# Fixed places of a state-space layer's side work in a dense matmul stream: some groups' state products and turned outputs stand one to three triples later

## The chip, the cores and the metric

One core of a Trainium2 chip runs the whole program. The metric is the device time of one execution in microseconds, as the median of several runs. One execution before was also taken by the hardware profiler; all rows shown here come from that one. Names of engines in the rows: PE is TensorE, PEld its weight loads, DVE is VectorE, ACT is ScalarE, POOL is GpSimd, SP is SyncE, which issues DMAs.

## The reference, cut to what matters

A token sequence of 512 x 1024 goes through one Mamba-2 layer, then one differential-attention layer, all in float32. The change lies in the Mamba-2 layer, which has 8 groups of 4 heads, 64 wide, with a state of 128:

```python
zxbcdt = rms_norm(x, norm_g) @ w_in            # z, x/B/C of 8 groups, dt
xbc = silu(causal_depthwise_conv(xbc, conv_w, conv_b))
# per chunk of the scan, per group g:
cb = einsum("blgn,bsgn->blsg", c_c, b_c)
y_diag = einsum("blsgr,bsgrp->blgrp", cb[..., None] * decay, x_c)
y_off = einsum("blgn,bgrpn->blgrp", c_c, state) * exp(acs)[..., None]
new_state = state * exp(acs[:, -1]) + einsum("blgn,blgrp->bgrpn", b_c, x_c * to_end)
...
y = y + d_skip * xs
y = gated_group_rms_norm(y, z, gate_norm_g)    # per group: y * silu(z), normed
return x + y @ w_out
```

## The kernel before

Float32 products are made as three matmuls of split operands (a high and a low part, `hi` and `lo`): `mm3`, line 259, called a **triple** here. The layer's projections are one dense stream of triples with a right side of 512 columns. `first_layer` (line 579) walks it by `order_a`: "z0 g0 g1 z1 g2 g3 z2 g4 o0 g5 z3 g6 g7 o1 o2 o3". A `z` item projects gate columns for two groups (into `pz`, then ScalarE's `zs`), a `g` item projects and convolves the x, B and C of one group (`pg`, then a scaling and three steps on VectorE into `xc`, with ScalarE around them), an `o` item is part of the output projection. Most items are 64 triples in two segments of weights. The weights come by SP's queue into `raw` (line 194), ScalarE makes `whi` and VectorE `wlo` of them, four instructions each for a segment, into three buffers in turn.

The work of the scan for group g is the generator `ssd` (line 618). It stops at each `yield` and is resumed at a fixed place: a number of triples, counted from the end of the group's own `g` item, out of the table `PLACES` (line 40). The columns of that table are groups 0 to 7. Its steps on TensorE are:

- `cb`: four products `pcb`.
- `bt`: three transposes `pbt`, which ScalarE copies into `bt`.
- `xt`: four transposes into `pxt_0` and four into `pxt_1`, which VectorE multiplies into `xdt` and `dx`; GpSimd makes `xe` of `xdt` (line 651).
- `st`: the state products `psA` and `psB` with `xe`, then `pyd`. The states `hst` go from ScalarE's copy of `psA` over GpSimd (line 662), VectorE, GpSimd (line 666) to VectorE.
- `o1`, `o2`: the products of states, `po`. Behind them `dx` is added up (GpSimd, line 701), gated, squared on ScalarE, and scaled by ScalarE into `tmp`.
- `y0`: the **turned outputs**: four transposes into `pyt_0`, four into `pyt_1`; ScalarE makes `yh` of each, VectorE `yl`.

The small PSUM tiles `pbt`, `pxt`, `psA`, `psB`, `pyd`, `po` and `pyt` share three banks in turn (`ss_bank`, line 96), so each of them waits until its bank's last tile has been read.

The decay tables `dec` have two buffers. `decays` (line 599) loads one by SP (line 606), GpSimd copies a piece (line 608), subtracts (line 610) and masks (line 611) it, four instructions each, and ScalarE takes the exponential of the whole table. The next load into a buffer waits until its last reader, among them line 666, is done.

TensorE's instructions run in the order in which they were recorded (`Ordered`, line 55; for all of them the profile shows line 70). The order on VectorE, ScalarE, GpSimd and SP is chosen by a scheduler when the program is built, and is then as fixed.

Of the kernel before, what the change touches and what calls it, by code (L numbers as in the profile page):

```python
# [38 lines left out]

PLACES = {  # L40
# [7 lines left out]
    "y2": (None,) * 7 + (72,),  # L48
}

# [1170 lines left out]
```

## Time and profile before

| what | value |
| --- | --- |
| median of 3 runs | 705.75 us (705.56 to 706.2) |
| profiled execution | 707.18 us, its span 705.4 us |
| TensorE busy | 696.1 us, 99% of the span |
| VectorE busy | 524.2 us, 74% |
| ScalarE busy | 426.3 us, 60% |
| GpSimd busy | 116.1 us, 16% |
| mean granted clock of TensorE | 0.998 |

The profile's times count from the start of the span. [...] Ends of matmuls are modelled, so a matmul's row of 0.39 us overlaps the next one, which starts 0.23 us after it.

### The profile page before, as it was taken

The page shows a single profiled execution, that of the slowest core. Times are in us where ns is not written, and L with a number is a line of the kernel's source. Part 1 is how long each engine was busy: PE and PEld are TensorE (multiplying, and loading weights), DVE is VectorE, ACT ScalarE, POOL GpSimd, SP SyncE. Part 2 cuts the span into 40 slices and gives each one's busy share as a digit, 9 for nine tenths or more (in the row PEclk, how much of TensorE's full clock was granted, in tenths as well). Part 3 has the DMA queues.
Part 4 walks back from the last instruction along what each step waited for, and adds up shares of the span by engine and source line. Part 5 has one row for each costly group of instructions (what it writes and reads, how often), then busy time and mean ns, then how long its engine had stood idle before and what let it go on. Part 6 is the DMA issues. An engine that isn't in the chain of part 4 may idle for free.

```text
span 705.4 us, 10468 instructions
## 1 busy us (share of the span) xinstructions
PE 696.1 (99%) x3838; PEld 580.7 (82%) x3838; DVE 524.2 (74%) x1181; ACT 426.3 (60%) x931; POOL 116.1 (16%) x158
## 2 busy tenths in 40 slices
PE   8999999999999999999999999999999999999996
PEld 7888788888878888888888888888888888888884
DVE  5499967799489679569995757557778757787776
ACT  6859663573654547536635258567777667665546
POOL 0008242502406025042110101000000000000002
PEclk9999999999999999999999999999999999999999
DMA  8654314214125323313222111513112221130103
GB/s 293 257 193 170 120 60 135 105 61 179 42 79 180 105 76 120 110 70 120 64 84 94 60 60 53 194 60 113 67 60 77 80 83 61 60 106 14 31 1 119
DMA packets 13491, 70.85 MB, mean 100 GB/s; under 512 B 1792, under 2 KB 3328, under 8 KB 6016
## 3 DMA queue, kind: packets, MB, share of 16 engines
q1 hardware_dynamic: 13008, 69.90, 27.6%
q8 instruction: 30, 0.49, 0.3%
q10 hardware_dynamic: 432, 0.28, 0.1%
q14 instruction: 21, 0.17, 0.1%
HBM read 68.02 MB, written 2.16 MB: 99 GB/s over the span
## 4 chain that ended last, share of the span: by engine, by line
PE 78%; DVE 8%; ACT 5%; DMA 4%; issue 3%; POOL 2%; SPq 0%; ACTq 0%; POOLq 0%; DVEq 0%
PE po L70 16%; PE pg L70 14%; PE pt L70 8%; PE pq L70 6%; PE pk L70 6%; PE pv L70 6%; PE pz L70 6%; PE pb L70 3%; DMA raw<-in_w_in 3%; PE sc L70 3%; DVE wlo L70 2%; ACT whi L70 2%; PE pc L70 2%; PE pyd L70 2%; DVE xc L70 1%
## 5 line engine op out<-in xcount | busy, mean ns | idle before, releaser
L70 DVE SCALAR_TENSOR_TENSOR wlo<-raw,prm,whi 128x512 fp32r<-128x512 f32 (+1 forms) x240 | 149.3, 672 | 54.0 <-ACT whi L70 53.7
L70 ACT ACTIVATE whi<-raw,prm 128x512 fp32r<-128x512 f32 (+1 forms) x240 | 133.2, 629 | 46.7 <-PE pg L70 12.0
L70 PE MATMUL pg<-a_hi,whi 128*128 128x512 f32 x256 | 102.8, 402 | 0.0
L70 PE MATMUL pg<-a_hi,wlo 128*128 128x512 f32 x256 | 99.9, 390 | 0.0
L70 PE MATMUL pg<-a_lo,whi 128*128 128x512 f32 x256 | 99.7, 389 | 0.0
L70 DVE SCALAR_TENSOR_TENSOR xc<-pg,prc,xc 128x511 f32<-128x511 f32 (+2 forms) x96 | 70.9, 743 | 12.3 <-ACT xc L70 11.2
L70 PEld LDWEIGHTS pg<-a_hi,wlo 128*128 128x128 f32 x256 | 48.1, 188 | 10.3
L70 PEld LDWEIGHTS pg<-a_hi,whi 128*128 128x128 f32 x256 | 48.2, 188 | 9.6 <-ACT zs L70 0.2
L70 PEld LDWEIGHTS pg<-a_lo,whi 128*128 128x128 f32 x256 | 48.1, 188 | 9.4
L70 PE MATMUL po<-whi,yh 128*128 128x512 f32 x128 | 51.2, 400 | 0.0
L70 PE MATMUL pz<-whi,a_hi 128*128 128x512 f32 x128 | 49.7, 397 | 0.3 <-ACT a_hi L70 0.3
L70 PE MATMUL po<-whi,yl 128*128 128x512 f32 x128 | 49.9, 390 | 0.0
L70 PE MATMUL po<-wlo,yh 128*128 128x512 f32 x128 | 49.9, 390 | 0.0
L70 PE MATMUL pz<-whi,a_lo 128*128 128x512 f32 x128 | 48.9, 390 | 0.0
L70 PE MATMUL pz<-wlo,a_hi 128*128 128x512 f32 x128 | 48.9, 389 | 0.0
L1026 POOL TENSOR_TENSOR ot<-x_tok,fg 128x512 f32<-128x512 f32 x4 | 5.0, 1284 | 246.8 <-DVE x_tok L70 246.8
L70 ACT ACTIVATE xc<-xc 128x512 f32<-128x512 f32 x32 | 20.2, 630 | 40.5 <-DVE xc L70 36.7
L70 ACT ACTIVATE xc<-pg,prc 128x512 f32<-128x512 f32 x32 | 24.8, 774 | 28.3 <-DVE pg L70 27.9
L70 DVE CUSTOM_DVE_ANT_0 s<-sc,bias 128x128 f32<-128x128 f32 (+3 forms) x64 | 29.4, 488 | 16.0 <-PE sc L70 15.5
L70 ACT ACTIVATE s<-s,mx 128x128 f32<-128x128 f32 (+3 forms) x64 | 35.6, 557 | 9.1 <-DVE mx L70 8.9
L651 POOL TENSOR_TENSOR xe<-xdt,tok 128x256 f32<-128x256 f32 x24 | 14.0, 613 | 159.3 <-DVE xdt L70 159.3
L70 ACT ACTIVATE tmp<-dx 128x256 f32<-128x256 f32 x32 | 13.1, 410 | 36.8 <-DVE dx L70 36.8
(237 smaller groups left out, 1651.1 us busy)
## 6 DMA issues: line engine op xcount, KB each, us to landing
raw<-in_w_in SPq DMA_DIRECT2D x22, 1024.0 KB, 4.9
raw<-in_w_kvqg SPq DMA_DIRECT2D x16, 1024.0 KB, 4.8
dec<-acs_d SPq DMA_DIRECT2D x8, 1024.0 KB, 5.1
raw<-in_w_out SPq DMA_DIRECT2D x8, 1024.0 KB, 4.9
raw<-in_w_bo SPq DMA_DIRECT2D x4, 1024.0 KB, 4.8
x_tok<-in_x SPq DMA_DIRECT2D x4, 512.0 KB, 9.0
out<-ot SPq DMA_DIRECT2D x6, 256.0 KB, 2.1
raw<-in_w_in SPq DMA_DIRECT2D x4, 256.0 KB, 4.9
```

The source lines that it names most:

```text
L70: i = op(*args, **kw)
L651: GP.tensor_tensor(out=xe[:, c], in0=xdt[:, c], in1=toe_tok[:, c, hs].unsqueeze(2).to_broadcast([P, R, HD]), op=ALU.mult)
L1026: GP.tensor_tensor(out=o, in0=y, in1=f, op=ALU.mult)
```

## The change

Fourteen of the table's numbers change. `st` of groups 0, 2 and 6 stands one or two triples later, `o1` and `o2` of group 0 three, `bt` of groups 1, 2, 3 and 6 two or three, `y0` of groups 0, 1, 2, 5 and 7 one to three. `cb` and `xt` keep their places.

```diff
--- before.py
+++ after.py
@@ -39,12 +39,12 @@
 
 PLACES = {
     "cb": (10, 2, 14, 14, 5, 5, 14, 12),
-    "bt": (10, 29, 21, 44, 35, 25, 21, 37),
+    "bt": (10, 32, 23, 47, 35, 25, 23, 37),
     "xt": (18, 35, 31, 52, 43, 36, 31, 43),
-    "st": (27, 47, 37, 63, 53, 47, 38, 53),
-    "o1": (31, 47, 46, 63, 53, 47, 46, 53),
-    "o2": (31, 52, 46, 69, 60, 52, 46, 58),
-    "y0": (61, 85, 76, 99, 89, 85, 69, 69),
+    "st": (29, 47, 39, 63, 53, 47, 39, 53),
+    "o1": (34, 47, 46, 63, 53, 47, 46, 53),
+    "o2": (34, 52, 46, 69, 60, 52, 46, 58),
+    "y0": (64, 87, 79, 99, 89, 87, 69, 70),
     "y2": (None,) * 7 + (72,),
 }
```

TensorE executes the same instructions in another order. The scheduler gives the other engines other orders as well. In the following rows the numbers behind a tile's name are counters, and some shift with the change (`tmp_797` and `tmp_810` are the same tile of group 0); a minus stands ahead of a row of before, a plus ahead of a row of after.

VectorE, behind group 0's `st`. Here `hst` and `dx` belong to group 0's states, `pg_2` and `xc` to the convolution of group 1, `wlo` to a later segment's weights:

```order
 L70 SCALAR_TENSOR_TENSOR wlo_655<-raw_652,prm,whi_654 128x512 x4
+L70 TENSOR_TENSOR pg_2_728<-pg_2_728,ar_row 128x512
+L70 SCALAR_TENSOR_TENSOR xc_790<-pg_2_728,prc,xc_790 128x511
+L70 SCALAR_TENSOR_TENSOR xc_790<-pg_2_728,prc,xc_790 128x510
 L70 TENSOR_TENSOR hst_757<-psA_758,hst_757 128x256
-L70 TENSOR_TENSOR dx_702<-pyd_1_799,dx_702 128x512
-L70 TENSOR_TENSOR hst_757<-psB_792,hst_757 128x256
-L70 TENSOR_TENSOR dx_702<-pyd_0_798,dx_702 128x512
-L70 TENSOR_TENSOR pg_2_728<-pg_2_728,ar_row 128x512
+L70 TENSOR_TENSOR dx_702<-pyd_1_812,dx_702 128x512
+L70 SCALAR_TENSOR_TENSOR xc_790<-pg_2_728,prc,xc_790 128x509
+L70 TENSOR_TENSOR dx_702<-pyd_0_811,dx_702 128x512
```

The scaling of `pg_2` and two convolution steps now stand ahead of the first `hst` add, the third one behind `dx`.

GpSimd, over the making of the third decay table, `dec_1217`, and the adds of group 0's `dx`:

```order
-L701 TENSOR_TENSOR dx_702<-dx_702,tmp_797 128x256
 L608 COPY dec_1217<-dec_1217 128x8
-L610 TENSOR_TENSOR dec_1217<-dec_1217,tok 128x512 x2
-L701 TENSOR_TENSOR dx_702<-dx_702,tmp_797 128x256 x2
-L610 TENSOR_TENSOR dec_1217<-dec_1217,tok 128x512 x2
-L611 AFFINE_SELECT dec_1217<-dec_1217 128x512 x4
-L651 TENSOR_TENSOR xe_1104<-xdt_1053,tok 128x256 x3
+L701 TENSOR_TENSOR dx_702<-dx_702,tmp_810 128x256
+L610 TENSOR_TENSOR dec_1217<-dec_1217,tok 128x512 x4
+L611 AFFINE_SELECT dec_1217<-dec_1217 128x512 x3
+L701 TENSOR_TENSOR dx_702<-dx_702,tmp_810 128x256 x2
+L611 AFFINE_SELECT dec_1217<-dec_1217 128x512
```

The copy of the table stands ahead of the first add; the second and third add stand behind the four subtractions and three of the four masks, and not between the subtractions.

ScalarE, around group 0's turned outputs and group 1's `bt`; `zs` are gates, `whi_1070` four pieces of weights:

```order
 L70 ACTIVATE zs_2_0_1028<-pz_2_990,ar_col 128x256
 L70 ACTIVATE zs_2_1_1030<-pz_2_990,ar_col 128x256
-L70 CAST yh_889<-pyt_0_891 128x512
-L70 CAST yh_889<-pyt_1_892 128x512
-L70 COPY bt_1051<-pbt_1047 128x384
 L70 ACTIVATE whi_1070<-raw_1068,prm 128x512 x4
 L70 ACTIVATE zs_3_0_1064<-pz_3_1003,ar_col 128x256
 L70 ACTIVATE zs_3_1_1066<-pz_3_1003,ar_col 128x256
+L70 COPY bt_1048<-pbt_1044 128x384
+L70 CAST yh_923<-pyt_0_925 128x512
+L70 CAST yh_923<-pyt_1_926 128x512
```

The three drains, `yh` twice and `bt`, stand behind the four `whi` and two more `zs`, with `bt` first.

TensorE, around group 2's turned outputs (`pyt`) and group 3's `pbt`; the minus rows of the same three stand nine matmuls, three triples, ahead of this piece:

```order
 L70 MATMUL pg_1_1860<-a_lo,whi_1599 128x512
 L70 MATMUL pg_1_1860<-a_hi,wlo_1600 128x512
+L70 MATMUL pbt_1882<-ident,xc_1420 128x128 x3
+L70 MATMUL pyt_0_1734<-ident,tmp_1628 128x128 x4
+L70 MATMUL pyt_1_1735<-ident,tmp_1628 128x128 x4
 L70 MATMUL pg_1_1860<-a_hi,whi_1599 128x512
 L70 MATMUL pg_1_1860<-a_lo,whi_1599 128x512
```

The eleven transposes stand behind three further triples of `pg_1`, in the same order among themselves. Group 0's `pyt` and group 1's `pbt` move in the same way by three triples, to three triples ahead of group 1's `pxt`.

## Rows read from the trace of the kernel before

**Rows 1.** Table by windows, whole core: stretch, length, each engine's busy us (instructions), granted clock, DMA share.

```profile
6.30:702.50 696.20, 691.63 (x3821) 576.64 (x3819) 523.06 (x1179) 423.40 (x925) 115.29 (x151) 1.00 0.28 99
702.60:705.40 2.80, 0.00 (x0) 0.00 (x0) 0.00 (x0) 0.00 (x0) 0.00 (x0) 0.50 0.46 158
```

**Rows 2.** TensorE's waits: waiting, releaser; total us, times, longest us.

```profile
PE psA L70 <- POOL xe L651: 0.4, 1, 0.4
...
PE pyt L70 <- ACT tmp L70: 0.3, 1, 0.3
```

**Rows 3.** Timeline of TensorE, `st` of groups 0 and 2: start, us, instruction, count.

```profile
73.56 0.39 PE L70 MATMUL pg<-a_hi,wlo 128*128 128x512 f32 x1
...
78.18 0.50 PE L70 MATMUL pg<-a_hi,whi 128*128 128x512 f32 x1
...
162.47 0.39 PE L70 MATMUL pz<-whi,a_lo 128*128 128x512 f32 x1
...
166.10 0.50 PE L70 MATMUL pz<-whi,a_hi 128*128 128x512 f32 x1
```

**Rows 4.** Timeline of TensorE, turned outputs of groups 0 and 2.

```profile
103.68 1.03 PE L70 MATMUL pyt<-ident,tmp 128*128 128x128 f32 x8
...
104.80 0.48 PE L70 MATMUL pz<-whi,a_hi 128*128 128x512 f32 x1
...
194.97 0.49 PE L70 MATMUL pbt<-ident,xc 128*128 128x128 f32 x3
...
197.52 0.47 PE L70 MATMUL pg<-a_hi,whi 128*128 128x512 f32 x1
```

**Rows 5.** Timeline of ScalarE, scaling ahead of group 2's turned outputs.

```profile
195.24 1.71 ACT L70 ACTIVATE tmp<-dx,y_y 128x256 f32<-128x256 f32 x4
```

**Rows 6.** Chain of waits between 102 and 116 us: start, us, what.

```profile
107.12 2.04 PE pg L70 x9
109.16 0.87 PE pxt L70 x8
```

**Rows 7.** Timeline of GpSimd, 72 to 100 us.

```profile
73.72 1.76 POOL L651 TENSOR_TENSOR xe<-xdt,tok 128x256 f32<-128x256 f32 x3 [5.28 <-DVE xdt L70]
...
87.34 0.19 POOL L608 COPY dec<-dec 128x8 f32<-128x8 f32 x1 [3.22 <-DMA dec<-acs_d]
...
94.23 2.39 POOL L611 TENSOR_SCALAR_AFFINE_SELECT dec<-dec 128x512 f32<-128x512 f32 x4
```

**Rows 8.** Timeline of VectorE, the add of `hst` in group 0.

```profile
78.61 0.41 DVE L70 TENSOR_TENSOR hst<-psA,hst 128x256 f32<-128x256 f32 x1
```

**Rows 9.** Page, part 5, VectorE's convolution steps: count, busy, mean ns, idle before.

```profile
L70 DVE SCALAR_TENSOR_TENSOR xc<-pg,prc,xc 128x511 f32<-128x511 f32 (+2 forms) x96 | 70.9, 743 | 12.3 <-ACT xc L70 11.2
```

**Rows 10.** Timeline of SP's queue, load of a decay table.

```profile
79.74 0.33 SPq L606 DMA_DIRECT2D dec<-acs_d  x1
```

**Rows 11.** Instructions touching `acs_d`: its transfers, issue to landing.

```profile
DMA to landing us min/median/max: 1.4/4.8/7.5
```

**Rows 12.** Timeline of ScalarE, 93 to 110 us.

```profile
93.93 1.28 ACT L70 ACT_TABLE_LOAD   x1
96.65 1.93 ACT L70 ACTIVATE dec<-dec 128x2056 f32<-128x2056 f32 x1 [1.44 <-POOL dec L611]
...
101.12 1.70 ACT L70 ACTIVATE tmp<-dx,y_y 128x256 f32<-128x256 f32 x4
...
105.17 0.82 ACT L70 ACTIVATE zs<-pz,ar_col 128x256 f32<-128x256 f32 x2
105.89 1.06 ACT L70 CAST yh<-pyt 128x512 fp32r<-128x512 f32 x2
106.83 0.50 ACT L70 COPY bt<-pbt 128x384 f32<-128x384 f32 x1
107.20 2.58 ACT L70 ACTIVATE whi<-raw,prm 128x512 fp32r<-128x512 f32 x4
```

**Rows 13.** Timeline of VectorE, `yl` of group 0.

```profile
106.50 1.29 DVE L70 TENSOR_TENSOR yl<-pyt,yh 128x512 fp32r<-128x512 f32 x2 [0.29 <-ACT yh L70]
```

## The prediction

> **What bounds the kernel now.** I read the table by windows first. Over the 696 us between the first microseconds and the last matmul TensorE is busy 691.63 us, at a granted clock of 1.00 [rows 1]. So the kernel is a stream of matmuls, and only two things can change its time: TensorE work added or removed, or holes in that stream. The change adds and removes no TensorE instruction, so everything here is about holes. The list of waits comes next. Besides two at the program's very start it holds two, both in the first layer: the products of group 0's states wait 0.4 us for a GpSimd product, and the turned outputs of one group wait 0.3 us for ScalarE [rows 2]. These entries understate the holes, because a matmul's end is modelled late. I size a hole by comparing start to start against the same block elsewhere.
>
> For group 0's states, the last dense matmul starts at 73.56 and the next one behind the block at 78.18, which is 4.62 us apart. For group 2 the same block lies between starts at 162.47 and 166.10, 3.63 us apart [rows 3]. **Hole one is 0.99 us.** For the turned outputs, eight `pyt` and three `pbt` transposes with nothing late take from 103.68 to 104.80, 1.12 us. At group 2's outputs they take from 194.97 to 197.52, 2.55 us [rows 4]. **Hole two is 1.43 us.** There the transposes keep pace with four ScalarE copies that run from 195.24 to 196.95 [rows 5].
>
> The unit of a place is a dense triple, three matmuls. The chain shows 9 of them in 2.04 us [rows 6], so one triple is 0.68 us.
>
> **Group 0's `st`, two triples later: -1.0 us.** The block would start 1.36 us after 73.79 (73.56 plus 0.227 for one matmul), at 75.15. GpSimd makes the three `xe` pieces from 73.72 to 75.48 [rows 7], about 0.59 each, so the two that `psA` reads are there at 74.9 and the third just as `psB` begins. The hole goes whole. If GpSimd slipped by half a microsecond, 0.5 of it would stay.
>
> **What hangs on that block's new place.** VectorE's order changes behind it. Before, the add of `hst` stands right behind four `wlo` and runs at 78.61 [rows 8]. Now the scaling of `pg_2` and two steps of the convolution stand ahead of it (the order of VectorE shows this), each convolution step 743 ns [rows 9], with a ScalarE step between. Taking the four at some 0.6 to 0.75 us each makes the add about 2.6 us late. TensorE hardly feels it: the block with `o1`, group 1's `cb` and `o2` starts at 75.15 + 3.5 + 5 x 0.68 = 82.05, its last two products, which need the second `hst` add, come more than a microsecond into it, and that add ends near 83.7; between 0 and 0.5 us could be missing, and I take 0, since a hole there would only shorten the wait of the next part. But the second `hst` product on GpSimd frees the buffer into which the next decay table is loaded, so SP's issue of that load, at 79.74 before [rows 10], moves to about 82.3. How long it then takes is open: these loads take 1.4 to 7.5 us, 4.8 in the middle [rows 11]. Before, this one was the slow one (79.74 to GpSimd's copy at 87.34 [rows 7]), issued right behind a weight load on SP. Issued 2.6 us later it finds that load mostly through, so I take the middle: landed at 87.1, as before. The slow end, 89.8, is a rival below.
>
> **Group 0's `y0` and group 1's `bt`, three triples later, with `xt` not moved: +3.7 us.** This is the largest term, and it is a new wait. Before, six triples lie between `pbt` and `pxt`, which starts at 109.16 by the chain [rows 6]; now three, 2.04 us. `pxt_0` needs the bank that ScalarE's copy `bt` empties, and `pxt_1` the bank that VectorE's `yl` of `pyt_0` empties, which itself waits for ScalarE's `yh`. Before, ScalarE did `yh` at 105.89 and `bt` at 106.83, ahead of the four `whi` at 107.20 [rows 12]. In the new order `bt`, `yh`, `yh` stand behind those four `whi` (2.58) and the two `zs` behind them (0.72 to the next start).
>
> When does ScalarE get there? GpSimd's new order puts the adds of `dx` 2 and 3 behind the four subtractions and three of the four selects. Before, GpSimd was busy without a gap from 87.34 to 96.62 [rows 7], 9.3 us; one add of about 0.7 us that ran earlier comes in as well. From 87.1 this ends at 96.8 to 97.1, the last add one select (2.39 / 4 = 0.6) before that, at 96.2 to 96.5. Then come a VectorE product and a ScalarE square, some 1 us, and a table load (1.28), so the exponential starts at about 98.6 and not at 96.65 [rows 12]. From there the old row gives 4.47 us to the `tmp` copies (101.12). One 0.54 us step has moved ahead of it, so 3.93: `tmp` from 102.5 to 104.2. Now in steps: four `whi` 2.5 to 106.7, `zs` 0.7 to 107.4, four `whi` 2.5 to 109.9, `zs` 0.7 to 110.6, `bt` 0.45 to 111.1, the first `yh` 0.5 to 111.6, `yl` 0.65 (half of 1.29 [rows 13]) to 112.25, and the second four transposes 0.44 (half of 0.87 [rows 6]) to 112.7.
>
> Undisturbed, with hole one gone, `pxt` would end at 109.0: 109.16 less 0.99, plus 0.87 for eight transposes [rows 6]. The wait is 112.7 less 109.0, **3.7 us**. Its upper bound is 4.4, if GpSimd ends 0.3 later and the square stands 0.4 behind other work. Its lower bound: even without a backlog ScalarE can't start the second four `whi` before the z segment whose buffer they take has ended. That was at 107.12 [rows 6]; less hole one and the 1.2 us of transposes that now come behind it, 104.9. Then 2.5 + 0.7 + 0.45 + 0.5 + 0.65 + 0.44 lead to 110.1, a wait of 1.1. I take 3.7, since each step of the long chain has its own row.
>
> **Group 2's `y0` and group 3's `bt`, three triples later: -1.4 us.** `pbt` goes to 197.0 in the old frame, and the four copies end at 196.95 [rows 5]. Hole two goes whole; if ScalarE came 0.7 us later here, half of it would stay. `pxt` of group 3 then stands five triples behind, 3.4 us, at 201.6. `pyt` ends at 198.2; `bt`, `yh` and `yl` (0.45, 0.5, 0.65), with a convolution step of 0.75 ahead of them on either engine, free its bank by 200.6 to 201.3: no new wait, but little to spare.
>
> **The rest: 0.** Group 1's `y0` and group 2's `bt`, as groups 5 and 6, move together by two triples, `pxt` eight triples behind them instead of ten; the drains behind `pyt` and `pbt` need under 4 us of those 5.4. `st` of groups 2 and 6 moves away from its producers. Group 7's `y0` moves by one triple, and its second half still follows its own drains.
>
> **Sum.** -1.0 + 3.7 - 1.4 = +1.3 us. The profiled execution took 707.18 (span 705.4), 1.43 above the median of 705.75; there the sum gives 708.5, and against the median **707.0**. A measurement of this kernel tells about 0.2%, 1.4 us, from no change: 704.3 to 707.2 is the same.
>
> **Rivals.** *The forecast's own case*, a wait at group 1's `pxt` of 1.1 to 4.4 us: -1.3 to +2.0, so 704.4 to 707.8. Chance 0.68: 0.44 of it within 0.2%, 0.24 slower, since the sum lies close to that bound.
>
> *The two holes close and nothing opens.* It would need ScalarE to come to `bt` about as early as before in spite of its order. Against it stands the fixed order; for it, that before, ScalarE was through with `yh` and `bt` at 107.3 [rows 12], 1.8 us ahead of `pxt`. Price: -1.0 - 1.4 = -2.4, so 703.3. Chance 0.14.
>
> *The decay load takes its long time from its later issue.* It lands at 89.8, 2.6 us after what I took, and GpSimd, the exponential and the whole ScalarE chain go with it; it decides as soon as the landing passes 87.5. +1.3 + 2.6 = +3.9, so 709.6. For it: the 7.5 us that this very load took before. Chance 0.10.
>
> *The wait is long enough for TensorE's clock to fall.* [...] Chance 0.08. [...]
>
> **How the numbers follow.** Faster 0.14 (the second case), same 0.44, slower 0.42 (0.24 of the forecast's case, 0.10 and 0.08). The range takes the forecast's case and the second one, 0.82: from 703.2 to 708.2, the upper end with 0.4 for what may stay of hole two. It leaves out the two slower rivals.
>
> **What would show it.** In the list of waits of the changed kernel `psA` is gone, and `pxt` of group 1 stands there for ScalarE's `bt` and VectorE's `yl` with 3 to 4 us in sum. On ScalarE's timeline `bt` and `yh` stand behind the second four `whi`, at about 111. The exponential starts near 98.6. Start to start, group 2's outputs take 1.1 us and not 2.55. If no `pxt` wait is there, the second case is right and my reading of ScalarE's order fails. If GpSimd's copy of the decay table comes after 88, the load was late. If the granted clock dips behind the wait, the last rival holds.

## The result and the profile after

| | median, us | span of the profiled execution, us |
| --- | --- | --- |
| before | 705.88 (705.51 to 706.94, 6 runs) | 705.4 |
| after | 710.08 (708.06 to 711.25, 6 runs) | 706.3 |

The ratio after to before is 1.0053, with an interval of 1.0042 to 1.0065: slower by about 4 us, where the forecast was 1.3 us and its range ended at 708.2. The profiled execution of before, at 707.18 us, lies above all six of its runs. That of after (span 706.3) is the shortest of its six, at a mean clock of 0.998. The other five had spans of 707.7 to 709.5 at a mean clock of 0.995 or 0.996. So this first profile shows the change with the clock held; what the other five have beside it is told by e1 below.

TensorE's waits in the profiled execution of after (waiting, releaser, total us, times, longest us). Beside two at the program's start the list holds only these; the two of [rows 2] are gone:

```profile
PE pxt L70 <- ACT bt L70: 2.3, 1, 2.3
...
PE pxt L70 <- DVE yl L70: 0.6, 1, 0.6
```

TensorE's timeline of after, at the three places that answer to [rows 3] and [rows 4] (start, us, instruction, count):

```profile
74.94 0.39 PE L70 MATMUL pg<-a_hi,wlo 128*128 128x512 f32 x1
...
78.57 0.50 PE L70 MATMUL pg<-a_hi,whi 128*128 128x512 f32 x1
...
107.76 0.39 PE L70 MATMUL pg<-a_hi,wlo 128*128 128x512 f32 x1
110.45 0.66 PE L70 MATMUL pxt<-ident,xc 128*128 128x128 f32 x4 [2.30 <-ACT bt L70]
111.66 0.66 PE L70 MATMUL pxt<-ident,xc 128*128 128x128 f32 x4 [0.56 <-DVE yl L70]
112.07 0.47 PE L70 MATMUL pg<-a_hi,whi 128*128 128x512 f32 x1
...
112.84 0.40 PE L70 MATMUL pg<-a_hi,whi 128*128 128x512 f32 x1
...
199.30 0.49 PE L70 MATMUL pbt<-ident,xc 128*128 128x128 f32 x3
...
200.42 0.48 PE L70 MATMUL pg<-a_hi,whi 128*128 128x512 f32 x1
```

Group 0's `st`: from 74.94 to 78.57, 3.63 us, against 4.62 in [rows 3]. Hole one is gone. Group 1's `pxt`: from the last dense matmul at 107.76 to the next at 112.07, 4.31 us; undisturbed that stretch is 1.02 us (108.52 to 109.54 in e6, a later profile of before, whose rows stand there). So TensorE waits 3.29 us there, in two pieces, 2.30 and 0.56 by the rows' own count. Group 2's outputs: from 199.30 to 200.42, 1.12 us, against 2.55 in [rows 4].

GpSimd in after, the copy of the decay table and the last two adds of `dx`, against [rows 7]:

```profile
86.51 0.54 POOL L608 COPY dec<-dec 128x8 f32<-128x8 f32 x1 [4.91 <-DMA dec<-acs_d]
...
93.70 1.43 POOL L701 TENSOR_TENSOR dx<-dx,tmp 128x256 f32<-128x256 f32 x2
```

ScalarE in after, against [rows 12]:

```profile
98.04 1.92 ACT L70 ACTIVATE dec<-dec 128x2056 f32<-128x2056 f32 x1
...
101.99 1.70 ACT L70 ACTIVATE tmp<-dx,y_y 128x256 f32<-128x256 f32 x4
...
106.76 2.55 ACT L70 ACTIVATE whi<-raw,prm 128x512 fp32r<-128x512 f32 x4
...
109.92 0.47 ACT L70 COPY bt<-pbt 128x384 f32<-128x384 f32 x1
110.28 1.09 ACT L70 CAST yh<-pyt 128x512 fp32r<-128x512 f32 x2
```

The table lands no later than before (copy at 86.51, before 87.34), though its load was issued later. The last add ends at 95.13, behind the subtractions and three of the masks; the exponential starts at 98.04, `tmp` at 101.99, the second four `whi` at 106.76, and only then `bt` at 109.92 and `yh` at 110.28.

Windows of after across the wait (stretch, length, busy us of TensorE and its weight loads, VectorE, ScalarE, GpSimd, then the granted clock):

```profile
108.00:110.40 2.40, 0.15 (x1) 0.00 (x0) 2.25 (x4) 2.40 (x7) 0.00 (x0) 1.00 0.85 287
110.40:112.00 1.60, 0.99 (x7) 0.76 (x8) 1.08 (x2) 0.97 (x2) 0.00 (x0) 1.00 0.99 307
```

In this one execution the clock stays at 1.00 through the wait.

### The profile page after: what moved, and what is told of

Same layout as the page of the kernel before. It is cut to its first block, busy times and chain, and to the rows that moved or that the text cites. A ratio compares the mean times of both kernels' runs of the same rounds, so it can differ in the third digit from the quotient of the medians.

```text
span 706.3 us, 10474 instructions
## 1 busy us (share of the span) xinstructions
PE 695.3 (98%) x3838; PEld 581.3 (82%) x3838; DVE 524.0 (74%) x1181; ACT 426.9 (60%) x931; POOL 117.6 (17%) x158
## 4 chain that ended last, share of the span: by engine, by line
PE 82%; issue 6%; DMA 3%; ACT 3%; DVE 3%; POOL 2%; SPq 0%; ACTq 0%; POOLq 0%
PE pg L70 18%; PE po L70 16%; PE pt L70 8%; PE pq L70 6%; PE pk L70 6%; PE pv L70 6%; PE pz L70 6%; PE pb L70 3%; PE sc L70 3%; PE pc L70 2%; PE pyd L70 2%; DMA x_tok<-in_x 1%; POOL dec L611 1%; DMA xt<-in_x_t 1%; PE pyt L70 1%
```

## The experiments

Runs e1, e5 and e6 are a kernel unchanged; the others are edits of the table of places alone. Theory A: the long runs of after come from TensorE's clock, which falls in the wait at `pxt`. Theory B: they come from a late decay load. Theories C and D, from the fifth run on, are on the size of the gain. C: the profiled execution of before was a long one, and most executions of before lack one of its two holes. D: both holes are always there.

**e1, the changed kernel again**

> The changed kernel once more. In its profiled execution group 1's pxt waited 3.3 us in all (its block took 4.17 us, 0.88 undisturbed), the granted clock stayed at 1.00, and the span was only 0.9 us over that of before; the timed runs were longer, at a mean clock of 0.996 and not 0.998. Theory A (the clock falls in that wait): again a median near 710, runs above 709 with a mean clock of 0.995 or 0.996, and a profile of such a run shows a granted clock below 1.00 in the microseconds behind the wait. Theory B (the decay load lands late in most runs): the long runs keep the clock of 0.998, or the profile shows GpSimd's copy of the table behind 88 us and a longer wait at pxt.

Measured: median 710.0 (709.33 to 711.26, 6 runs), all at a mean clock of 0.994 to 0.996; ratio 1.006 (1.0039 to 1.0081). This time the profiled execution was one of these, with a span of 708.1. Its windows, same columns as above:

```profile
109.00:111.00 2.00, 0.00 (x0) 0.00 (x0) 2.00 (x4) 2.00 (x5) 0.00 (x0) 1.00 0.76 266
111.00:112.00 1.00, 0.78 (x4) 0.71 (x4) 0.34 (x2) 1.00 (x3) 0.00 (x0) 0.58 0.97 401
...
113.00:114.00 1.00, 1.00 (x5) 0.90 (x4) 1.00 (x3) 0.00 (x0) 0.00 (x0) 0.50 0.87 360
114.00:115.00 1.00, 1.00 (x4) 0.77 (x4) 1.00 (x3) 0.00 (x0) 0.06 (x1) 0.71 1.03 434
115.00:116.00 1.00, 1.00 (x7) 0.79 (x5) 0.46 (x1) 0.00 (x0) 1.00 (x2) 1.00 0.18 74
```

TensorE's timeline in it:

```profile
108.10 0.39 PE L70 MATMUL pg<-a_hi,wlo 128*128 128x512 f32 x1
111.22 2.32 PE L70 MATMUL pxt<-ident,xc 128*128 128x128 f32 x8 [2.73 <-ACT bt L70]
113.19 0.78 PE L70 MATMUL pg<-a_hi,whi 128*128 128x512 f32 x1
113.77 0.63 PE L70 MATMUL pg<-a_lo,whi 128*128 128x512 f32 x1
...
114.61 0.40 PE L70 MATMUL pg<-a_hi,whi 128*128 128x512 f32 x1
```

GpSimd's copy of the decay table, and ScalarE's `bt`:

```profile
87.06 0.75 POOL L608 COPY dec<-dec 128x8 f32<-128x8 f32 x1 [4.70 <-DMA dec<-acs_d]
...
110.69 0.48 ACT L70 COPY bt<-pbt 128x384 f32<-128x384 f32 x1
```

From 109 to 111 us TensorE does nothing. At about 111.2 the granted clock goes to 0.50; by 115 it is 1.00 again. The eight transposes and the matmuls behind them run in between: the first dense one is followed 0.58 us later by the second (113.19, 113.77), where it is 0.32 us in after's first profile and 0.23 from one dense matmul to the next. From the last dense matmul to the first transpose it takes 3.12 us (108.10 to 111.22), in after's first profile 2.69 (107.76 to 110.45): 0.43 us are a longer wait. From there to the second triple's start at 114.61 it takes 3.39 us, in the first profile 2.39 (110.45 to 112.84): 1.00 us is the clock's. A third difference lies ahead of the wait: the block of group 0's `o1`, group 1's `cb` and group 0's `o2` takes 2.30 us start to start here (82.11 to 84.41) and 2.00 there, 0.30 more. The three make 1.73 of the 1.8 us between the two spans. So Theory A is shown for this execution; the decay table was copied at 87.06, 0.55 us behind the time of after's first profile, which speaks against B. For the other long runs of after the mean clock says the same, but what makes some of them up to 1.4 us longer than this one is open. Of the 23 runs of before beside e1 one, of 709.27 us, has a mean clock of 0.995 too; where its clock fell no profile shows.

**e2, group 1's `xt` three triples later**

```diff
-    "xt": (18, 35, 31, 52, 43, 36, 31, 43),
+    "xt": (18, 38, 31, 52, 43, 36, 31, 43),
```

> The changed kernel with group 1's xt three triples later (38 for 35), so that pxt stands six triples behind pbt as it did before. ScalarE's order up to bt and yh is the same as in the changed kernel. pxt then waits for the same drains (bt at 110.4, yl at 111.6), but only 1.1 to 1.2 us. Theory A: such a wait leaves the clock alone, mean clock 0.998: before's median 705.9 - 2.4 + 1.2 = 704.7. Theory B: the late load adds its 3 us here as well: about 708.

Measured: 706.42 (705.89 to 707.01, 12 runs), mean clocks of 0.997 to 0.999; ratio 1.0008 (0.9997 to 1.0018). TensorE's timeline and the window across the wait:

```profile
110.95 0.66 PE L70 MATMUL pxt<-ident,xc 128*128 128x128 f32 x4 [0.69 <-ACT bt L70]
112.16 0.66 PE L70 MATMUL pxt<-ident,xc 128*128 128x128 f32 x4 [0.56 <-DVE yl L70]
```

```profile
111.00:112.50 1.50, 0.94 (x7) 0.71 (x8) 1.08 (x2) 0.87 (x2) 0.00 (x0) 1.00 1.09 284
```

The drains come between those of the two profiles of after (`bt` at 110.43), but dense work covers most of the time: two waits of 0.69 and 0.56 us remain, the clock stays at 1.00 and 3.6 us of the loss are gone. By its clock and its waits this is Theory A's case. The time alone does not decide it: it lies 1.7 us above A's 704.7 and 1.6 below B's 708. The miss of A's number is the first sign that something else in the sum was wrong.

**e3, group 1's `xt` two triples earlier**

```diff
-    "xt": (18, 35, 31, 52, 43, 36, 31, 43),
+    "xt": (18, 33, 31, 52, 43, 36, 31, 43),
```

> The changed kernel with group 1's xt two triples earlier (33): the drains come at the same time, so the wait grows by 1.36 us to some 4.7 us, and so does the whole. With a clock that holds: 705.9 + 0.9 + 1.4 = 708.2. Theory A: the clock falls in every run, 0.996 or less, 711 to 712. Theory B: 711.4 (after's 710.1 + 1.4) at a mean clock of 0.998.

Measured: 712.22 (711.01 to 712.73, 6 runs), mean clocks of 0.993 to 0.995; ratio 1.0086 (1.0068 to 1.0105). The wait and the windows in its profiled execution:

```profile
111.42 2.32 PE L70 MATMUL pxt<-ident,xc 128*128 128x128 f32 x8 [4.95 <-ACT bt L70]
```

```profile
110.00:111.00 1.00, 0.00 (x0) 0.00 (x0) 1.00 (x2) 1.00 (x4) 0.00 (x0) 0.96 0.93 393
111.00:112.00 1.00, 0.58 (x3) 0.58 (x4) 0.34 (x2) 1.00 (x4) 0.00 (x0) 0.50 1.06 451
...
117.00:118.00 1.00, 1.00 (x4) 0.80 (x3) 0.00 (x0) 0.00 (x0) 0.00 (x0) 0.63 0.00 0
```

A longer wait (4.95 us) costs 2.2 us more than e1 in the median, of which 1.36 are the two triples that now stand behind it. The clock is at 0.50 from 111 until past 117, longer than in e1, although dense work runs again from 113.39 on. From the first transpose to the fifth triple's start it takes 6.83 us (111.42 to 118.25), in after's first profile 4.45: here the clock costs 2.4 us. A's 711 to 712 is missed by 0.2 us; a clock that holds (708.2) and B's mean clock of 0.998 are far off.

**e4, group 0's `y0` and group 1's `bt` put back**

```diff
-    "bt": (10, 32, 23, 47, 35, 25, 23, 37),
+    "bt": (10, 29, 23, 47, 35, 25, 23, 37),
-    "y0": (64, 87, 79, 99, 89, 87, 69, 70),
+    "y0": (61, 87, 79, 99, 89, 87, 69, 70),
```

> The changed kernel with group 0's y0 and group 1's bt back at their old places (61, 29), all other moves kept. ScalarE's order then has bt and yh ahead of the second four whi again. pxt finds its banks free; pyt stands at 102.7 and waits for the tmp copies, which end at 103.7: about 1 us. Theory A: 705.9 - 2.4 + 1.0 = 704.5 at a clock of 0.998. Theory B: the late load pushes the tmp copies and so the wait at pyt to 3 to 4 us: 707 to 708.

Measured: 706.03 (705.35 to 707.37, 12 runs), mean clocks of 0.997 to 0.999; ratio 1.0004 (0.9993 to 1.0015). TensorE's timeline:

```profile
103.26 0.49 PE L70 MATMUL pbt<-ident,xc 128*128 128x128 f32 x3
...
105.27 0.47 PE L70 MATMUL pz<-whi,a_hi 128*128 128x512 f32 x1
...
109.47 1.04 PE L70 MATMUL pxt<-ident,xc 128*128 128x128 f32 x8
110.26 0.47 PE L70 MATMUL pg<-a_hi,whi 128*128 128x512 f32 x1
```

The transposes of the outputs take 2.01 us start to start (103.26 to 105.27) where 1.12 is undisturbed, so the wait for `tmp` is 0.9 us as expected; `pxt` (109.47 to 110.26) waits for nothing. With these two numbers of the table put back, the loss of the change is gone within the noise. Theory B's wait of 3 to 4 us did not come, but here as well the time was 1.5 us over A's sum.

**e5 and e6, the kernel before, profiled again**

> The kernel before, profiled again. Two runs of the changed table without the long wait (e2, e4) came out 1.5 us above what the sum says against the median of before, though against the profiled execution of before they agree with it. Theory C: the profiled execution of before (span 705.4) was a long one, and most runs (spans of 703.5 to 703.9) lack one of its two holes; a profile with a span under 704 then shows group 2's outputs in 1.1 us, or psA of group 0 without its wait. Theory D: both holes are always there and the difference lies elsewhere (the first microseconds, the end): then such a profile shows both, 4.6 us and 2.55 us start to start.

> The kernel before, profiled a third time, with the same expectations as for the second: under theory C a span near 703.6 comes with one hole of the two missing, a span near 705.4 with both; under theory D both holes stand in either.

Measured: spans of 704.4 (706.17 us) and 703.8 (705.6 us). In e6, around group 2's outputs, TensorE's timeline has

```profile
194.79 0.49 PE L70 MATMUL pbt<-ident,xc 128*128 128x128 f32 x3
...
195.91 0.48 PE L70 MATMUL pg<-a_hi,whi 128*128 128x512 f32 x1
```

and around group 0's `st` and group 1's `pxt`

```profile
73.46 0.39 PE L70 MATMUL pg<-a_hi,wlo 128*128 128x512 f32 x1
...
77.94 0.50 PE L70 MATMUL pg<-a_hi,whi 128*128 128x512 f32 x1
...
108.52 0.39 PE L70 MATMUL pg<-a_hi,wlo 128*128 128x512 f32 x1
...
109.54 0.48 PE L70 MATMUL pg<-a_hi,whi 128*128 128x512 f32 x1
```

It is 1.12 us from 194.79 to 195.91: **hole two is not there**. It is not in e5 either. The load of the decay table ahead of it, in the profile that the prediction used and then in e6 (SP's issue, GpSimd's copy of the landed table):

```profile
168.78 0.33 SPq L606 DMA_DIRECT2D dec<-acs_d  x1
```

```profile
175.32 0.19 POOL L608 COPY dec<-dec 128x8 f32<-128x8 f32 x1 [6.57 <-DMA dec<-acs_d]
```

```profile
168.25 0.33 SPq L606 DMA_DIRECT2D dec<-acs_d  x1
```

```profile
173.24 0.20 POOL L608 COPY dec<-dec 128x8 f32<-128x8 f32 x1 [5.02 <-PE pcb L70]
```

And the loads between 165 and 176 us, in the first profile and in e6 (KB, median us to landing):

```profile
raw<-in_w_out SPq DMA_DIRECT2D x1, 1024.0 KB, 6.3
dec<-acs_d SPq DMA_DIRECT2D x1, 1024.0 KB, 6.4
```

```profile
raw<-in_w_out SPq DMA_DIRECT2D x1, 1024.0 KB, 4.7
dec<-acs_d SPq DMA_DIRECT2D x1, 1024.0 KB, 4.8
```

In the first profile a 1 MB weight load took 6.3 us and the table behind it 6.4; in e6 they took 4.7 and 4.8. The issue stood 0.53 us later there. GpSimd's copy came 6.5 us behind the issue there and 5.0 here, and ScalarE's whole chain to `tmp` moved with it, from 195.24 [rows 5] to 193.18. In e5 the table took 5.8 us, and the outputs were still not held up. Hole one varies as well: 0.99 us in the first profile, 0.85 in e6 (4.48 less 3.63), 0 in e5, where TensorE was itself late, by a wait of 1.6 us near 29 us. Theory C holds for hole two. Why the two loads took a third longer in one execution is open.

**e7 and e10, group 2's `y0` and group 3's `bt` alone**

```diff
-    "bt": (10, 29, 21, 44, 35, 25, 21, 37),
+    "bt": (10, 29, 21, 47, 35, 25, 21, 37),
-    "y0": (61, 85, 76, 99, 89, 85, 69, 69),
+    "y0": (61, 85, 79, 99, 89, 85, 69, 69),
```

> The kernel before with one part of the change alone: group 2's y0 at 79 and group 3's bt at 47. By the prediction hole two goes: -1.4 us, 704.2 against before's 705.6. Theory C with hole two missing in most runs of before: no change, 705.4 to 705.8, and never a run at 707. Theory D: 704.2.

> Group 2's y0 and group 3's bt alone once more, on the same chip as the best candidate. If hole two stands in some executions of before only, when a decay load lands late, this takes off the long runs and little from the median: 0.1 to 0.6 us under before, and e9 lies below it by hole one, 0.3 to 1.0.

Measured: 705.39 (704.49 to 705.8, 12 runs), ratio 0.9986 (0.9976 to 0.9996); and 705.6 (704.97 to 706.28, 11 runs), ratio 0.9992 (0.9983 to 1.0001). The highest of these 23 runs is 706.28. Of the 44 runs of before beside them 14 are above that, up to 708.75 and at mean clocks of 0.997 to 0.999, while the lowest are 705.23 and 704.94. So this part takes off long runs and little from the median, as C has it: 0.1 to 0.6 us and not 1.4. That the long runs of before are those with hole two is inferred, since they have no profile.

**e8, group 0's `st`, `o1` and `o2` alone**

```diff
-    "st": (27, 47, 37, 63, 53, 47, 38, 53),
-    "o1": (31, 47, 46, 63, 53, 47, 46, 53),
-    "o2": (31, 52, 46, 69, 60, 52, 46, 58),
+    "st": (29, 47, 37, 63, 53, 47, 38, 53),
+    "o1": (34, 47, 46, 63, 53, 47, 46, 53),
+    "o2": (34, 52, 46, 69, 60, 52, 46, 58),
```

> The kernel before with another part alone: group 0's st at 29 and its o1 and o2 at 34; y0 stays at 61 and group 1's bt at 29. Hole one goes (-1.0). The decay table comes about 2 us later, so the tmp copies end near 103.7 and pyt, at 102.7, waits about 1 us for them: near 0 in sum, 705.6, by theory D. By theory C with hole one missing in most runs of before, +1.0: 706.6.

Measured: 705.88 (705.26 to 707.95, 12 runs) beside 705.95 of before; ratio 0.9998 (0.9989 to 1.0007). TensorE's timeline at group 0's outputs, which stand at their old place:

```profile
102.75 0.49 PE L70 MATMUL pbt<-ident,xc 128*128 128x128 f32 x3
...
104.81 0.47 PE L70 MATMUL pz<-whi,a_hi 128*128 128x512 f32 x1
```

2.06 us start to start, a wait of 0.9 us. What hole one gives, the wait for `tmp` takes back, as expected by D. C's 706.6 for a hole one missing in most runs did not come. The profiles bear it out: where group 0's `st` stands at its old place, hole one is there in four of five (0.99 us, 0.85 in e6, 0.36 in e7, 0.81 in e10, none in e5). Only hole two is missing in most.

**e9, the changed kernel with `bt` at its old place and `y0` one triple earlier**

```diff
-    "bt": (10, 32, 23, 47, 35, 25, 23, 37),
+    "bt": (10, 29, 23, 47, 35, 25, 23, 37),
-    "y0": (64, 87, 79, 99, 89, 87, 69, 70),
+    "y0": (63, 87, 79, 99, 89, 87, 69, 70),
```

> The changed kernel with group 1's bt back at 29 and group 0's y0 at 63 (one earlier than in the change); all other moves kept. ScalarE's order has bt and yh ahead of the second four whi again; pyt stands at 104.4, behind the tmp copies that end at 103.7, and pxt at 108.0, behind bt (about 107.3). So both holes of group 0 and group 1 are gone, and hole two with them. If the changed kernel's loss is that one wait and the clock that falls in it: before's median less hole one (0.3 to 1.0) and less what hole two is worth in the mean (0 to 0.6): 0.3 to 1.6 us faster than before, mean clock 0.998, no long wait in the list. If the moved states cost something of their own, it is no faster than before.

Measured: 705.5 (704.98 to 706.41, 11 runs), ratio 0.9993 (0.9984 to 1.0002). Its waits, beside the two at the program's start:

```profile
PE pxt L70 <- DVE yl L70: 0.3, 1, 0.3
```

No long wait, and the change's loss is gone: ScalarE's order has the drains ahead of the second four `whi` again (`bt` at 107.51, `whi` at 108.82). Its `tmp` copies start at 102.74, as late as e1's at 102.76, so the long wait comes from the order of the drains and not from the later chain alone. The gain is 0.2 us, under the 0.3 to 1.6 expected. `yl` still takes 0.3 us of it by holding `pxt`; where the rest of hole one's 0.85 us went is not shown. The run lies level with e10 and is not shown to be faster than before.

## Why the prediction was wrong, point by point

**Hole one** (-1.0) went as worked out: `psA` started at 75.17, worked out as 75.15. In e1, where GpSimd's `xe` ran 0.76 us later than in after's first profile, it went too.

**The late decay load.** It landed as taken: GpSimd's copy stood at 86.51 and, in e1, at 87.06, worked out as 87.1. It was issued 4.0 us behind a weight load and took 4.7 and 4.5 us (6.0 in e3), where before it was issued 1.0 us behind one and took 7.5. The rival of the long load did not happen in either profile of after.

**The wait at `pxt`** (+3.7) came by the chain that was worked out, and e1 met it almost step by step: the exponential at 98.81 (98.6), `tmp` at 102.76 (102.5), `bt` at 110.69 (110.6). Without the clock the wait there is 3.29 + 0.43 = 3.72 us. In after's first profile the same steps stood some 0.8 us earlier and TensorE 0.3, hence its 3.29. The mechanism, the place and the size were right.

**Hole two** (-1.4) is the first step that failed. The edit does take the hole away when it is there. But it was there in one of three profiles of before, since a decay load had taken 6.4 us. The prediction sized this term on one execution and then set the sum against the median. It even gave the number that should have stopped it: the profiled execution was 1.43 us above the median, as much as hole two. The term was worth 0.1 to 0.6 us in the median (e7, e10). Set against the profiled execution itself the sum comes out: -0.99 + 3.29 - 1.43 = +0.87 us, and the two spans differ by 0.9.

**The clock rival** (chance 0.08) is the second step. Its chance was the author's estimate, and the range left it out. But 11 of the 12 runs of after show the lower mean clock, e1 with a wait only 0.43 us longer than in the one that doesn't. With the clock held the change cost 2.5 us against e6 (706.3 to 703.8); the spans of the other 11 runs lie 1.3 to 3.2 us above that. The step that failed is the weight given to the clock of 1.00 over 696 us. The holes inside that stream were at most 1.43 us long, so it said nothing on one of three microseconds. The one idle stretch of such a length in the trace was the end of the program, and there the clock did fall [rows 1]. The prediction took the 696 us to end with the last matmul. That matmul starts at 698.73, so TensorE had been idle for some 3.4 us at 1.00 when the clock fell at about 702.6 (0.80 in the window of before from 702.5 to 702.6, 0.50 in the next tenth); in e1 it had been idle for 2.7 us, in e3 for 4.5, and in after's first profile 2.3 us passed without a fall. Behind the wait the windows of e1 and e3 show 0.50, which cost 1.00 us in e1 and 2.4 in e3. What decides whether a wait brings the clock down no run shows.

**The sum** with what was measured, e1 against e6: hole one -0.85 us; `pxt` from 108.10 to 113.19, 5.09, where 1.02 is undisturbed, +4.07; the first triple behind it 1.42 us (113.19 to 114.61) where it is 0.78 in e6, +0.64; `o1`, `cb` and `o2` +0.30; hole two 0. That is +4.16, and the spans differ by 4.3 (708.1 to 703.8). The medians differ by 4.2. Beside the forecast's +1.3 this is 1.4 for hole two, 1.0 for the clock, 0.3 for `o2` and 0.15 for a smaller hole one.

**The rest** (0) held nearly: no other wait of the changed kernel stands in its list. The products of group 0's `o2`, for which 0 to 0.5 us was given and 0 taken, cost 0 in after's first profile and 0.30 us in e1.

## What to carry to other kernels

When a profiled execution is longer than the median, look for what is special in it before its waits are counted as gains: a second profile of the unchanged kernel would have shown hole two to be absent. In a dense TensorE stream a new wait of a few microseconds is to be priced with the clock as well: here a wait of about 3 us cost 1.0 us more by it in one execution and nothing in another, a wait of 5 us cost 2.4. And moving a step in a fixed order moves what the other engines put ahead of it: three triples were enough to let four weight instructions and two gates go ahead of three short drains that TensorE needed.

## What the runs showed that was not expected

At one and the same place a wait of 2.69 us from the last dense matmul to the first transpose left the clock at 1.00 in one execution, and one of 3.12 us brought it to 0.50 for about 3.4 us in another (e1's windows, 111 to 115). What decided between these two is open: no run separates the length of the wait from the moment at which it comes. A wait of 4.95 us brought some 6.8 us at 0.50 (e3's windows). Two DMAs of 1 MB one behind the other took 4.7 and 4.8 us in one execution of the kernel before and 6.3 and 6.4 in another.
